# HGRN and mLSTM step on one core: weight splits and feature products moved from GpSimd to VectorE, small copies to ScalarE, and v's gate weights placed behind evictions

## The chip, the cores and the metric

The kernel runs on one core of a Trainium2 chip. The metric is the time of one execution on the device in microseconds (us). Before the change the median of three runs is 1189.55 us (1186.49 to 1191.88). Five engines work beside each other, each on its own queue: TensorE (PE: matmuls and transposes; its weight loads are shown as PEld), VectorE (DVE), ScalarE (ACT), GpSimd (POOL) and SyncE (SP, which here issues the DMAs).

## The reference

One layer of a hybrid decoder, for a prompt of 1024 tokens and 8 samples of 8 tokens (1088 token columns in all), model width 1024. After an RMSNorm one input projection of width 7168 gives the inputs of two mixers; both are causal recurrences over the tokens.

```python
proj = rmsnorm(x, g_norm) @ w_in
xm, zm, om, fh, qh, ih, zh = split(proj)             # 7 parts of 1024
# mLSTM, 4 heads, dk 128, dv 256
xc = silu(causal_conv(xm)); q = xc @ w_q; k = xc @ w_k; v = xm @ w_v      # per head
gates = concat(q, k, v) @ w_gate + b_gate            # input gate and forget gate of each head
hm = mlstm_scan(q, k, v, gates)                      # matrix memory C, normaliser n, stabiliser m
hm = (layernorm(hm) * sigmoid(om) + m_skip * xc) * silu(zm)
# HGRN2, 8 heads, dk = dv = 128
f = lb + (1 - lb) * sigmoid(fh); k = (1 - lb) * sigmoid(-fh); q = silu(qh)
oh = hgrn2_scan(q, k, ih, log f)                     # S_t = diag(f_t) S_(t-1) + k_t i_t ; o_t = S_t^T q_t
oh = rmsnorm(oh) * silu(zh)
y = rmsnorm(x + concat(hm, oh) @ w_out, g_final)
```

The new states of both mixers are outputs as well.

## The kernel before

A product of float32 accuracy is made of three matmuls: each operand is split into `hi`, a copy in a rounded 32-bit format, and `lo = raw - hi`. Lines 94, 95 and 96 are the three matmuls hi x hi, lo x hi, hi x lo of a projection, for tiles of 384, 384 and 320 token columns into the PSUM tile `mm`. The weights of the input projection come in 56 blocks of 128 columns. For each block one DMA on SP's queue brings `wraw` (three buffers), ScalarE casts `whi`, GpSimd subtracts `wlo`, both at L147 in `w_split`.

In time the program has these stages: the norm and split of x (to some 38 us); the front, which projects the mLSTM inputs, runs the conv (`front_conv`, sums `Y`), and makes v, q and k with the gate weights folded into the weights (`qkv_prep`, `front_v`, `front_qk`; to some 208 us); then a row of jobs H0 M0 H1 M1 H2 M2 H3 M3 H4 H5 H6 H7, where H is the scan of one HGRN head (`hgrn_main`) and M that of one mLSTM head (`mlstm_main`); and the output projection (from some 1020 us).

In `qkv_prep` v's gate weights take three steps on TensorE: four transposes of w_v (L395, evicted as `wT`), two matmuls with w_gate (L399, evicted as `gv`), two small transposes (L404), whose result VectorE splits into `wqh` and `wql`, columns of the weights of v (L406, L407). Between them only the dependences and the scheduler's costs set the place.

In the jobs TensorE's order is fixed by the code. `weave` runs a job as a generator whose `yield`s give the time of the other engines' work in us; between two yields it puts that much of the next job's input projection (the side blocks, "fillers" here), scaled by the projection's time over `HEAD[kind] + extra`. Each job takes exactly 48 pieces of the side work. VectorE, ScalarE, GpSimd and SP follow the scheduler's order, one in-order queue each.

An H job works in levels n = 1, 2, 4, 8, 16, 32, 64. For each level VectorE builds the factors `QK` from queries, keys and running products of f (`products`, L1016, L950; `Sf` L1019 and `f` L1021 carry the running products; level 1 uses `Q` L983, `K` L947, L998 to L1000). A burst of small matmuls of 32x32 blocks (L101) then gives the scores, and they are copied into the score matrix `A`, through the small tile `A32` for n up to 16. There are three bursts: level 1 and 2; `lower` (2, 4 and 8); `upper` (16, 32 and 64). After `upper` a predicated copy on VectorE fills `A32`, six copies (L1058 and L1060) bring A32 to A, and six copies on ScalarE (L1066) bring the rest from PSUM. TensorE's transposes L1123 follow; the second group of them takes the PSUM buffer that those copies read.

`mixed` finishes the mLSTM features of the job before: a DMA brings `xcr`, VectorE makes a fused product (L846), GpSimd multiplies by `zm` (L848), and a DMA stores it to `mixd`. It runs within the next H job, behind the products of the levels, as `late` work.

Of the kernel before, what the change touches and what calls it, by code (L numbers as in the profile page):

```python
# [13 lines left out]
ALU = mybir.AluOpType  # L14
# [16 lines left out]
def hybrid_step(  # L31
# [46 lines left out]
    def f32(ap):  # L78
        return ap.bitcast(F32)
# [61 lines left out]

    def w_split(key):
        raw = wq[key]
        hi = wp.tile([P, 1024], F32R, tag="whi", name=nm("whi"))
        lo = wp.tile([P, 1024], F32R, tag="wlo", name=nm("wlo"))
        wq[key] = (hi.rearrange("p (k c) -> p k c", c=P), lo.rearrange("p (k c) -> p k c", c=P))
        return S.copy(hi, raw), G.tensor_tensor(lo, raw, f32(hi), op=ALU.subtract)  # L147

# [11 lines left out]
    bidx = {b: i for i, b in enumerate(blocks)}  # L160

    def blk_load(i):
        if i < len(blocks):
            kind, j = blocks[i]
            o = boff[kind] + j * P
            return w_load(("w", i), w_in[0, :, o:o + P].rearrange("(k p) c -> p k c", p=P))

    def blk_split(i):
        if i < len(blocks):
            return w_split(("w", i))  # L170

# [201 lines left out]
    def vcols(w):  # L373

        return w[:, 512:1040].rearrange("p (a c) -> p a c", c=264)

    def qkv_prep(h):

# [13 lines left out]
        for b in range(2):  # L392
            for a in range(2):
                o, i = 512 + a * 256 + b * P, b * 2 + a
                PE.transpose(pt[:, i * P:(i + 1) * P], wr[:, o:o + P], ident)  # L395
        V.tensor_copy(wT[:, :512], pt)
        pg = ps_o()
        for b in range(2):
            PE.matmul(pg[:8, :256], lhsT=wgr[:, 8 + 2 * h + b, :], rhs=wT[:, b * 256:(b + 1) * 256],  # L399
                      start=b == 0, stop=b == 1)  # L400
        gv = sp.tile([P, 256], F32, tag="hn", name=nm("gv"), bufs=3)
        V.tensor_copy(gv[:8, :], pg[:8, :256])
        for a in range(2):
            PE.transpose(pg[:, 256 + a * 8:264 + a * 8], gv[:8, a * P:(a + 1) * P], ident[:8, :8])  # L404
        pgv = pg[:, 256:272].rearrange("p (a c) -> p a c", c=8)
# [35 lines left out]

    fr = {}

    def front_conv(h, fts):

        cw, cb = par("conv_w"), par("conv_b")
        items, st = [], []
        for ft in fts:
            XB = unit("XB")
# [6 lines left out]
            def evac(c, t0, n, ps, XB=XB, sv=sv, mh=mh, ml=ml):  # L456
                m = min(n, TP - t0)
                S.copy(mh[:, t0:t0 + m], ps[:, :m])
                S.copy(XB[:, 3 + t0:3 + t0 + m], ps[:, :m])  # L459
                V.tensor_tensor(ml[:, t0:t0 + m], ps[:, :m], f32(mh[:, t0:t0 + m]), op=ALU.subtract)  # L460
                if m < n:
                    S.copy(sv[:, :, 3:11], ps[:, m:n].rearrange("p (b c) -> p b c", c=8))
                    S.copy(twice(mh[:, TP:U]), once(ps[:, m:n]))
                    V.tensor_tensor(twice(ml[:, TP:U]), once(ps[:, m:n]), twice(f32(mh[:, TP:U])), op=ALU.subtract)
# [79 lines left out]
    def gate_scan():  # L544
# [20 lines left out]
        V.tensor_tensor_scan(m, t1, y, initial=0.0, op0=ALU.add, op1=ALU.max)  # L565
        yield 5.5
        G.memset(t1, 1.0)
# [12 lines left out]
        nc.sync.dma_start(out=o_sm[0].rearrange("b h -> h b"), in_=msl[0:4, :])  # L580
        yield 5.5
        ps = ps_o()
# [82 lines left out]
    def mlstm_main(h):  # L665
# [176 lines left out]
        def mixed(a):  # L842
# [4 lines left out]
                                   op0=ALU.mult, op1=ALU.add)  # L847
            G.tensor_tensor(xc[:, :T], xc[:, :T], d["zm"][a][:, :T], op=ALU.mult)  # L848
            nc.sync.dma_start(out=mixd[ft], in_=xc[:, :T])
# [77 lines left out]
    def hgrn_main(h):  # L927
# [11 lines left out]
        def fold(Kn, n, second, ns):  # L939

            Knv = Kn[:, :512].rearrange("p (r c) -> p r c", c=P)
            for odd in range(2):
# [3 lines left out]
                if n == 1:  # L946
                    i = (G if second else V).tensor_copy(dst, ksrc)  # L947
                else:
# [32 lines left out]
        Q1 = unit("Q1")  # L981
        G.tensor_copy(hv(Q1, T, 1)[:, :, 0, :], hv(q, T, 1)[:, :, 0, :])
        q1 = V.tensor_tensor(hv(Q1, T, 1)[:, :, 1, :], hv(q, T, 1)[:, :, 1, :], hv(f, T, 1)[:, :, 1, :], op=ALU.mult)  # L983
# [41 lines left out]
        def level_run(group):  # L1025
# [24 lines left out]
            for n, o in outs:  # L1050
                if n <= 16:
                    small_out(ps, o, LEVELS.index(n) + 1, n)
                    if n == 16:

                        for j in range(4):
                            a = A[32 * j:32 * j + 32, 32 * j:32 * j + 1]
                            dst = bass.AP(a.tensor, a.offset, [a.ap[0], [256, 4], [224 - 64 * j, 2], [1, 32]])
                            G.tensor_copy(dst, A32[32 * j:32 * j + 32, 0:256].rearrange("p (r e c) -> p r e c", e=2, c=32))  # L1058
                        for g in range(2):
                            G.tensor_copy(A[64 * g:64 * g + 32, TP + 32 * g:TP + 32 * g + 32],  # L1060
                                          A32[64 * g:64 * g + 32, 256:288])
                else:
# [7 lines left out]
        for n in (2, 4, 8):  # L1070
            lower.append(products(n))
            if late:
                with tc.issue_after(getattr(lower[-1][3], "ins", lower[-1][3])):
                    late.pop(0)()
                yield 1.8
            yield 3.3
# [38 lines left out]
        level_run(upper)  # L1115
        yield 2.0
        KDt = unit("KDt")
# [415 lines left out]
```

## Time and profile before

| | |
|---|---|
| median of 3 runs | 1189.55 us (1186.49 to 1191.88) |
| profiled execution | 1189.85 us, span 1188.1 us, mean granted clock 0.985 |
| TensorE | busy 1130.5 us (95%), 9251 matmuls |
| VectorE | 782.3 us (66%), 1447 instructions |
| ScalarE | 441.1 us (37%), 973 |
| GpSimd | 381.9 us (32%), 504 |
| GpSimd's splits L147 | 56 of 2495 ns, 139.7 us |
| GpSimd's multiply L848 | 8 of 2727 ns, 21.8 us |

How it is read: in the waits, "PE lv L101 <- DVE QK L950" means that TensorE's instruction of line 101, which writes tile `lv`, waited for VectorE's of line 950, which writes `QK`. In a timeline a row gives the start, the duration, engine, line, operation, tiles and shapes, how many such instructions follow each other, and in brackets the idle time ahead of them and what ended it. "PEclk" is the share of the full clock that TensorE was granted in a window. H0 runs from about 208 to 298 us, H1's part up to its transposes from 363 to 412, H2's from 494 to 543, H3's from 626 to 675, H4's from 757 to 811.

### The profile page before, as it was taken

To read this page: it belongs to the slowest core of one execution; us is meant where nothing else is said; L and a number is where in the kernel's file an instruction comes from. 1 tells how busy PE (TensorE), PEld (TensorE's weight loads), DVE (VectorE), ACT (ScalarE), POOL (GpSimd) and SP (SyncE) were. 2 spreads that over 40 slices of the span, in tenths; PEclk is the share of its full clock that TensorE was granted. 3 is DMA by queue.
4 is the path that set the end of the run, shared out by engine and by line. 5 is a ranking of instruction groups with operands and counts; after the bars stand their busy time and mean duration, and the time that the engine had idled before them with its cause. 6 is when DMAs were issued, how large, how long until landed. Compare 5 with 4: busy or idle time off the path is not lost.

```text
span 1188.1 us, 22927 instructions
## 1 busy us (share of the span) xinstructions
PE 1130.5 (95%) x9251; PEld 1062.1 (89%) x9251; DVE 782.3 (66%) x1447; ACT 441.1 (37%) x973; POOL 381.9 (32%) x504
## 2 busy tenths in 40 slices
PE   5889999979999999999999999989999999999997
PEld 5789999979999899998999899979999997877886
DVE  4665454395778767794678667795959587643543
ACT  5455454325431343225331453232232344343322
POOL 4352434132534344343534343443333211100000
PEclk9989999989999999999999999998999999999999
DMA  8134243222323242323224232321221155476652
GB/s 264 42 127 147 101 160 102 73 55 90 100 80 115 71 165 75 116 80 118 80 76 144 77 131 76 118 84 58 59 59 51 59 175 152 144 232 166 210 178 100
DMA packets 154061, 133.88 MB, mean 113 GB/s; under 512 B 11440, under 2 KB 130156, under 8 KB 153955
## 3 DMA queue, kind: packets, MB, share of 16 engines
q1 hardware_dynamic: 153954, 132.41, 35.8%
q8 instruction: 73, 1.20, 0.4%
q14 instruction: 34, 0.27, 0.1%
HBM read 93.96 MB, written 38.43 MB: 111 GB/s over the span
## 4 chain that ended last, share of the span: by engine, by line
PE 54%; DVE 13%; DMA 5%; ACT 2%; issue 2%; POOL 0%; SPq 0%; POOLq 0%; DVEq 0%; ACTq 0%
PE mm L94 14%; PE mm L96 14%; PE mm L95 14%; DVE QK L950 3%; DVE Sf L1019 2%; DVE f L1021 2%; DMA xcr<-xcd 2%; DMA woraw<-in_w_out 2%; PE o L1169 1%; DMA mraw<-mixd 1%; DVE QK L1016 1%; PE o L1188 1%; PE o L95 1%; PE o L94 1%; PE o L96 1%
## 5 line engine op out<-in xcount | busy, mean ns | idle before, releaser
L94 PE MATMUL mm<-XH,whi 128*128 128x384 f32 (+1 forms) x1344 | 454.0, 338 | 6.5 <-DVE z L890 6.2
L95 PE MATMUL mm<-XL,whi 128*128 128x384 f32 (+1 forms) x1344 | 442.1, 329 | 0.0
L96 PE MATMUL mm<-XH,wlo 128*128 128x384 f32 (+1 forms) x1344 | 441.7, 329 | 0.0
L94 PEld LDWEIGHTS mm<-XH,whi 128*128 128x128 f32 x1344 | 255.6, 190 | 10.3 <-DVE z L890 6.3
L95 PEld LDWEIGHTS mm<-XL,whi 128*128 128x128 f32 x1344 | 255.7, 190 | 1.7 <-issue 1.3
L96 PEld LDWEIGHTS mm<-XH,wlo 128*128 128x128 f32 x1344 | 255.0, 190 | 0.0
L147 POOL TENSOR_TENSOR wlo<-wraw,whi 128x1024 fp32r<-128x1024 f32 x56 | 139.7, 2495 | 184.9 <-ACT whi L147 184.4
L147 ACT CAST whi<-wraw 128x1024 fp32r<-128x1024 f32 x56 | 58.8, 1051 | 146.7 <-PE mm L95 126.5
L96 PE MATMUL mm<-XH,mlo 128*128 128x512 f32 x144 | 56.4, 392 | 2.0 <-DVE mlo L1282 2.0
L94 PE MATMUL mm<-XH,mhi 128*128 128x512 f32 x144 | 57.2, 397 | 0.5 <-ACT mhi L1281 0.5
L950 DVE TENSOR_TENSOR QK<-hk,Sf 128x256 f32<-128x256 f32 x96 | 56.2, 625 | 0.0
L95 PE MATMUL mm<-XL,mhi 128*128 128x512 f32 x144 | 56.1, 390 | 0.0
L1281 ACT CAST mhi<-mraw 128x1024 fp32r<-128x1024 f32 (+1 forms) x32 | 31.8, 996 | 61.6 <-PE mm L95 42.0
L1350 POOL TENSOR_TENSOR rs<-rs,mhalf 128x1 f32<-128x1 f32 (+1 forms) x9 | 4.9, 543 | 149.5 <-DVE rs L1349 149.5
L1282 DVE TENSOR_TENSOR mlo<-mraw,mhi 128x1024 fp32r<-128x1024 f32 (+1 forms) x32 | 36.9, 1154 | 23.8 <-ACT mhi L1281 23.8
L460 DVE TENSOR_TENSOR xml<-mm,xmh 128x384 fp32r<-128x384 f32 (+1 forms) x24 | 12.1, 508 | 57.8 <-ACT XB L459 48.8
L1019 DVE TENSOR_TENSOR Sf<-Sf,f 128x512 f32<-128x512 f32 (+1 forms) x48 | 46.5, 969 | 0.1
L882 DVE TENSOR_SCALAR f<-f,OML,LB 128x384 f32<-128x384 f32 (+1 forms) x24 | 32.1, 1338 | 19.5 <-ACT f L880 19.3
L1021 DVE TENSOR_TENSOR f<-f 128x512 f32<-128x512 f32 (+1 forms) x48 | 42.2, 879 | 0.8
L1060 POOL COPY A<-A 32x32 f32<-32x32 f32 x16 | 14.3, 891 | 85.2 <-DVE A L977 84.8
L96 PE MATMUL mm<-woh,mlo 128*128 128x512 f32 x96 | 37.5, 391 | 0.5 <-DVE mlo L1282 0.5
L94 PE MATMUL mm<-woh,mhi 128*128 128x512 f32 x96 | 37.4, 389 | 0.0
(350 smaller groups left out, 2221.7 us busy)
## 6 DMA issues: line engine op xcount, KB each, us to landing
wraw<-in_w_in SPq DMA_DIRECT2D x56, 512.0 KB, 4.2
woraw<-in_w_out SPq DMA_DIRECT2D x16, 512.0 KB, 5.3
mraw<-mixd SPq DMA_DIRECT2D x16, 512.0 KB, 5.4
mraw<-mixd SPq DMA_DIRECT2D x16, 448.0 KB, 3.8
xcd<-XB SPq DMA_DIRECT2D x8, 544.0 KB
qkd<-qk SPq DMA_DIRECT2D x16, 272.0 KB, 4.4
xcr<-xcd SPq DMA_DIRECT2D x8, 544.0 KB
mixd<-xcr SPq DMA_DIRECT2D x8, 544.0 KB, 2.7
```

The costliest lines, as they stand in the source:

```text
L94: PE.matmul(out, lhsT=lh, rhs=rh, start=first, stop=False)
L95: PE.matmul(out, lhsT=lh, rhs=rl, start=False, stop=False)
L96: PE.matmul(out, lhsT=ll, rhs=rh, start=False, stop=last)
L147: return S.copy(hi, raw), G.tensor_tensor(lo, raw, f32(hi), op=ALU.subtract)
L460: V.tensor_tensor(ml[:, t0:t0 + m], ps[:, :m], f32(mh[:, t0:t0 + m]), op=ALU.subtract)
L882: V.tensor_scalar(f[:, s], f[:, s], scalar1=OML[:, h:h + 1], scalar2=LB[:, h:h + 1], op0=ALU.mult, op1=ALU.add)
L950: i = V.tensor_tensor(dst, ksrc, ssrc, op=ALU.mult)
L1019: V.tensor_tensor(hv(Sf, W, n)[:, :, 0, :], hv(Sf, W, n)[:, :, 0, :], hv(f, W, n)[:, :, 1, n - 1:n].to_broadcast([P, ng, n]), op=ALU.mult)
L1021: V.tensor_tensor(hv(f, W, n)[:, :, 1, :], hv(f, W, n)[:, :, 1, :], hv(f, W, n)[:, :, 0, n - 1:n].to_broadcast([P, ng, n]), op=ALU.mult)
L1060: G.tensor_copy(A[64 * g:64 * g + 32, TP + 32 * g:TP + 32 * g + 32], A32[64 * g:64 * g + 32, 256:288])
L1281: S.copy(hi[:, :w * n], raw[:, :w * n])
L1282: V.tensor_tensor(lo[:, :w * n], raw[:, :w * n], f32(hi[:, :w * n]), op=ALU.subtract)
```

## The change

The subtraction of 22 of the 56 weight splits moves from GpSimd to VectorE: those issued within H jobs (the job's own z block and the first two blocks of the next job). So does the multiply by `zm` in `mixed`. ScalarE takes from GpSimd the even half of `Q`, the second key copies of level 1, and the copies A32 to A. The yields of the gate scan, of the late work and behind the upper burst grow, and HEAD and `extra` with them. `behind` ties each of the three TensorE steps of v's gate weights, by a dependence without a semaphore, to an eviction `xml` of the projection that runs beside them: the first, the one at a third, the one ahead of two thirds.

```diff
-    def w_split(key):
+    def w_split(key, eng=G):
...
-        return S.copy(hi, raw), G.tensor_tensor(lo, raw, f32(hi), op=ALU.subtract)
+        return S.copy(hi, raw), eng.tensor_tensor(lo, raw, f32(hi), op=ALU.subtract)
...
+    v_splits = {8 + 4 * j + n for j, (kind, _) in enumerate(jobs) if kind == "H" for n in (3, 4, 5)}
...
-            return w_split(("w", i))
+            return w_split(("w", i), V if i in v_splits else G)
...
+    def behind(i, r):
+        tc.add_manual_dep(getattr(i, "ins", i), getattr(r, "ins", r).name, mybir.DependencyInfo(
+            mybir.DependencyClass.NoSync, mybir.DependencyReason.DATA), reason="behind")
...
-                PE.transpose(pt[:, i * P:(i + 1) * P], wr[:, o:o + P], ident)
+                behind(PE.transpose(pt[:, i * P:(i + 1) * P], wr[:, o:o + P], ident), evs[0])
...
-            PE.matmul(pg[:8, :256], lhsT=wgr[:, 8 + 2 * h + b, :], rhs=wT[:, b * 256:(b + 1) * 256],
-                      start=b == 0, stop=b == 1)
+            behind(PE.matmul(pg[:8, :256], lhsT=wgr[:, 8 + 2 * h + b, :], rhs=wT[:, b * 256:(b + 1) * 256],
+                             start=b == 0, stop=b == 1), evs[len(evs) // 3])
...
-            PE.transpose(pg[:, 256 + a * 8:264 + a * 8], gv[:8, a * P:(a + 1) * P], ident[:8, :8])
+            behind(PE.transpose(pg[:, 256 + a * 8:264 + a * 8], gv[:8, a * P:(a + 1) * P], ident[:8, :8]),
+                   evs[2 * len(evs) // 3 - 1])
...
-                V.tensor_tensor(ml[:, t0:t0 + m], ps[:, :m], f32(mh[:, t0:t0 + m]), op=ALU.subtract)
+                evs.append(V.tensor_tensor(ml[:, t0:t0 + m], ps[:, :m], f32(mh[:, t0:t0 + m]), op=ALU.subtract))
...
-        yield 5.5
+        yield 6.5
...
-        yield 5.5
+        yield 6.5
...
-            G.tensor_tensor(xc[:, :T], xc[:, :T], d["zm"][a][:, :T], op=ALU.mult)
+            V.tensor_tensor(xc[:, :T], xc[:, :T], d["zm"][a][:, :T], op=ALU.mult)
...
-                    i = (G if second else V).tensor_copy(dst, ksrc)
+                    i = S.copy(dst, ksrc) if second else V.tensor_copy(dst, ksrc)
...
-        G.tensor_copy(hv(Q1, T, 1)[:, :, 0, :], hv(q, T, 1)[:, :, 0, :])
+        S.copy(hv(Q1, T, 1)[:, :, 0, :], hv(q, T, 1)[:, :, 0, :])
...
-                            G.tensor_copy(dst, A32[32 * j:32 * j + 32, 0:256].rearrange("p (r e c) -> p r e c", e=2, c=32))
+                            S.copy(dst, A32[32 * j:32 * j + 32, 0:256].rearrange("p (r e c) -> p r e c", e=2, c=32))
...
-                            G.tensor_copy(A[64 * g:64 * g + 32, TP + 32 * g:TP + 32 * g + 32],
-                                          A32[64 * g:64 * g + 32, 256:288])
+                            S.copy(A[64 * g:64 * g + 32, TP + 32 * g:TP + 32 * g + 32], A32[64 * g:64 * g + 32, 256:288])
...
-                yield 1.8
+                yield 2.6
...
         level_run(upper)
-        yield 2.0
+        yield 3.4
...
-    HEAD = {"H": 47.2, "M": 48.2}
+    HEAD = {"H": 48.6, "M": 48.2}
...
-                extra = 3.6
+                extra = 5.2
             if i == 0:
-                main, extra = with_gates(main, gates), 12.0
+                main, extra = with_gates(main, gates), 14.0
```

Line numbers of the changed kernel are larger: by 2 at L239 to L351, 7 or 8 from L395 to L407, 10 from L460 to L1060, and 9 behind that.

**VectorE in H1, from the scores of level 1 to the products of level 8.** `xcr` is `mixed`'s tile (two of them, 4046 and 4092), `QK_4085` level 4, `QK_4139` level 8. Before:

```order
L1019 TENSOR_TENSOR Sf_3937<-Sf_3937,f_3550 128x272x2
L977 COPY_PREDICATED A_539_3935<-mk_366,lv_3990 128x144
L1021 TENSOR_TENSOR f_3550<-f_3550 128x272x2
L950 TENSOR_TENSOR QK_4085<-hk_3551,Sf_3937 128x64x4
L950 TENSOR_TENSOR QK_4085<-hk_3551,Sf_3937 128x4x16x4
L952 TENSOR_TENSOR QK_4085<-hk_3551,Sf_3937 128x64
L1016 TENSOR_TENSOR QK_4085<-hq_3552,f_3550 128x544
L1019 TENSOR_TENSOR Sf_3937<-Sf_3937,f_3550 128x136x4
L1021 TENSOR_TENSOR f_3550<-f_3550 128x136x4
L846 SCALAR_TENSOR_TENSOR xcr_4092<-xcr_4092,PAR,om_2929 128x1088
L1016 TENSOR_TENSOR QK_4139<-hq_3552,f_3550 128x512
L950 TENSOR_TENSOR QK_4139<-hk_3551,Sf_3937 128x32x8
```

After (L856 is L846, L858 is L848, L960 is L950, L1026 is L1016, L1029 is L1019, L1031 is L1021):

```order
L987 COPY_PREDICATED A_539_3935<-mk_366,lv_3990 128x144
L856 SCALAR_TENSOR_TENSOR xcr_4046<-xcr_4046,PAR,om_2683 128x1088
L1026 TENSOR_TENSOR QK_4085<-hq_3552,f_3550 128x544
L1029 TENSOR_TENSOR Sf_3937<-Sf_3937,f_3550 128x136x4
L858 TENSOR_TENSOR xcr_4046<-xcr_4046,zm_3152 128x1088
L856 SCALAR_TENSOR_TENSOR xcr_4092<-xcr_4092,PAR,om_2902 128x1088
L1031 TENSOR_TENSOR f_3550<-f_3550 128x136x4
L147 TENSOR_TENSOR wlo_4109<-wraw_3949,whi_4108 128x1024
L858 TENSOR_TENSOR xcr_4092<-xcr_4092,zm_3353 128x1088
L1026 TENSOR_TENSOR QK_4139<-hq_3552,f_3550 128x512
L960 TENSOR_TENSOR QK_4139<-hk_3551,Sf_3937 128x32x8
L960 TENSOR_TENSOR QK_4139<-hk_3551,Sf_3937 128x4x8x8
```

Two multiplies (L858) and a split (L147) now stand ahead of the products of level 8; another split stands ahead of the last piece of `hq`, in front of all the levels, and a third ahead of the job's end.

**ScalarE in H1, from the scan's values to the copies that TensorE's transposes wait for.** `A_539` with `A_3933` are A and A32, `lv_4367` the PSUM tile of the upper burst. Before:

```order
L1102 CAST Vs_4330<-V_4311 128x128
L1106 ACTIVATE VH_4331<-Vs_4330,CF 128x128 x4
L1107 ACTIVATE VL_4332<-Vs_4330,CF 128x128 x4
L1066 COPY A_3933<-lv_4367 32x4x32 x4
L1066 COPY A_3933<-lv_4367 64x4x64 x2
L634 ACTIVATE om_4271<-mm_4348 128x384
```

After (L1075 is L1066):

```order
L1111 CAST Vs_4330<-V_4311 128x128
L1115 ACTIVATE VH_4331<-Vs_4330,CF 128x128 x4
L1116 ACTIVATE VL_4332<-Vs_4330,CF 128x128 x4
L1068 COPY A_3933<-A_539_3935 32x4x2x32 x3
L1068 COPY A_3933<-A_539_3935 32x4x64
L1075 COPY A_3933<-lv_4367 32x4x32 x4
L1075 COPY A_3933<-lv_4367 64x4x64 x2
L644 ACTIVATE om_4271<-mm_4348 128x384
```

The four copies A32 to A (L1068) stand ahead of the six copies out of PSUM. The two small ones (L1070) stand earlier, behind the evictions of z.

**TensorE in H1, between the upper burst and the transposes** (L1123, now L1132; `mm_4436` is a side block's tile of 320 columns):

```order
 L95 MATMUL mm_4436<-XL,whi_4108 128x320
 L96 MATMUL mm_4436<-XH,wlo_4109 128x320
-L1123 MATMUL lv_4447<-CF,iT_3553 128x128 x4
-L1123 MATMUL lv_4453<-CF,iT_3553 128x128 x4
-L1123 MATMUL o_4459<-CF,iT_3553 128x128
+L94 MATMUL mm_4436<-XH,whi_4108 128x320
+L95 MATMUL mm_4436<-XL,whi_4108 128x320
+L96 MATMUL mm_4436<-XH,wlo_4109 128x320
+L94 MATMUL mm_4436<-XH,whi_4108 128x320
+L95 MATMUL mm_4436<-XL,whi_4108 128x320
+L96 MATMUL mm_4436<-XH,wlo_4109 128x320
+L1132 MATMUL lv_4453<-CF,iT_3553 128x128 x4
```

Six more fillers stand ahead of the transposes. In the same way six fillers of the next tile now stand ahead of the lower burst.

**TensorE in the front, head 0, at the end of its second block's projection** (`mm_539`) and the start of v (`mm_618`):

```order
 L95 MATMUL mm_539<-XL,whi_167 128x320
 L96 MATMUL mm_539<-XH,wlo_168 128x320
-L404 MATMUL o_609<-CF,gv_612 128x8 x2
-L395 MATMUL o_848<-CF,wqkv_719 128x128 x4
+L406 MATMUL o_609<-wT_602,front_341 8x256 x2
+L411 MATMUL o_609<-CF,gv_612 128x8 x2
 L94 MATMUL mm_618<-wqh_376,xmh_385 128x264
 L94 MATMUL mm_630<-wqh_376,xmh_385 128x264
-L399 MATMUL o_854<-wT_847,front_341 8x256 x2
 L95 MATMUL mm_618<-wql_377,xmh_385 128x264
```

L399 (now L406), which stood at the start of the projection, now stands right ahead of L404 (now L411) and of v's first matmuls. Head 1's transposes and L399 (o_848, o_854) leave this place for the projection that follows.

More of the change, by code (lines that the diff above doesn't have):

```diff
@@ L442, in hybrid_step @@
     fr = {}
+    evs = []
     def front_conv(h, fts):
@@ L447, in front_conv @@
         items, st = [], []
+        evs.clear()
         for ft in fts:
```

## The prediction

> **What bounds the kernel now.** I read the page first, then the waits of TensorE, then the timeline of TensorE, VectorE, GpSimd and ScalarE inside one HGRN job, and last the table by windows of the clock. The page says who sets the time:
>
> ```profile
> PE 1130.5 (95%) x9251; PEld 1062.1 (89%) x9251; DVE 782.3 (66%) x1447; ACT 441.1 (37%) x973; POOL 381.9 (32%) x504
> ```
>
> TensorE is busy for 95% of the span, and the change takes no matmul away. What it can win is TensorE's waiting, and time in which TensorE runs at half clock. The waits of TensorE (us in total, times, longest):
>
> ```profile
> PE lv L1123 <- ACT A L1066: 10.5, 5, 3.2
> PE lv L101 <- DVE QK L950: 7.9, 4, 2.2
> PE mm L94 <- DVE z L890: 6.2, 1, 6.2
> ```
>
> The first two are the ends of the two halves of an HGRN job: the burst of small products (L101) that waits for the factors QK of level 8, and the transposes (L1123) that wait until ScalarE has copied the upper burst out of its PSUM tile. They fall in heads 0 to 4; H5 to H7 show none. One job, head 1, on TensorE:
>
> ```profile
> 387.80 0.48 PE L101 MATMUL lv<-QK 128*32 128x32 f32 x32 [1.97 <-DVE QK L950]
> ...
> 401.68 1.22 PE L101 MATMUL lv<-QK 128*32 128x32 f32 x96
> ...
> 403.98 0.31 PE L94 MATMUL mm<-XH,whi 128*128 128x320 f32 x1
> ...
> 404.86 0.60 PE L1123 MATMUL lv<-CF,iT 128*128 128x128 f32 x4
> 406.63 0.66 PE L1123 MATMUL lv<-CF,iT 128*128 128x128 f32 x4 [1.18 <-ACT A L1066]
> ```
>
> In head 0 the transposes wait less, so that 10.5 - 0.75 = 9.75 us of that row belong to H1 to H4:
>
> ```profile
> 274.69 0.66 PE L1123 MATMUL lv<-CF,iT 128*128 128x128 f32 x4 [0.75 <-ACT A L1066]
> ```
>
> The waits also cost clock. In the windows below the columns are length, busy us of PE, PEld, DVE, ACT, POOL, then PEclk. They are cut where the granted clock changes:
>
> ```profile
> 384.69:388.10 3.41, 1.44 (x114) 1.09 (x113) 3.41 (x3) 0.49 (x1) 2.77 (x2) 1.00 0.44 168
> 388.10:391.51 3.41, 3.41 (x32) 3.35 (x19) 3.38 (x8) 0.00 (x0) 0.00 (x0) 0.50 0.56 154
> 538.29:541.70 3.41, 3.41 (x15) 3.41 (x15) 0.58 (x2) 1.05 (x4) 0.00 (x0) 0.50 0.02 5
> 801.11:804.52 3.41, 2.56 (x11) 2.56 (x12) 1.09 (x3) 3.01 (x9) 0.25 (x1) 0.50 0.00 1
> 804.52:807.94 3.42, 3.42 (x16) 3.42 (x15) 0.30 (x1) 0.00 (x0) 0.00 (x0) 0.50 0.00 0
> 667.99:671.40 3.41, 1.59 (x12) 1.59 (x13) 0.00 (x0) 3.31 (x11) 1.11 (x3) 1.00 0.08 19
> 671.40:674.80 3.40, 3.40 (x29) 3.40 (x28) 1.92 (x6) 0.26 (x1) 0.00 (x0) 1.00 0.02 5
> ```
>
> After a window with 1.44 us of busy TensorE the next runs at 0.50; after one with 1.59 it does not. So a wait of 1.97 us already costs half of the next 3.41 us, 1.7 us. Such losses in H1 to H4: 1.7 (H1, 388.10), 1.7 (H2, 538.29), and in H4 half of 2.56 and of 3.42, 3.0; together 6.4 us.
>
> [...]
>
> **Why VectorE is late.** VectorE's timeline in H1, from the queries to the products of the next levels:
>
> ```profile
> 365.31 2.17 DVE L983 TENSOR_TENSOR Q<-hq,f 128x544 f32<-128x544 f32 x1
> ...
> 374.01 2.92 DVE L1019 TENSOR_TENSOR Sf<-Sf,f 128x544 f32<-128x544 f32 x1
> ...
> 379.24 0.71 DVE L1019 TENSOR_TENSOR Sf<-Sf,f 128x544 f32<-128x544 f32 x1
> ...
> 382.50 5.24 DVE L950 TENSOR_TENSOR QK<-hk,Sf 128x256 f32<-128x256 f32 x2
> ...
> 389.45 0.75 DVE L950 TENSOR_TENSOR QK<-hk,Sf 128x256 f32<-128x256 f32 x2
> ...
> 397.86 2.77 DVE L1021 TENSOR_TENSOR f<-f 128x512 f32<-128x512 f32 x1
> 400.66 1.29 DVE L1086 TENSOR_TENSOR hq<-hq,f 128x1088 f32<-128x1088 f32 x1
> ```
>
> The same operation on the same shape takes 2.92 and 0.71, 5.24 and 0.75. The long ones end 0.3 to 0.6 us behind the end of a GpSimd instruction:
>
> ```profile
> 364.50 2.39 POOL L147 TENSOR_TENSOR wlo<-wraw,whi 128x1024 fp32r<-128x1024 f32 x1 [0.96 <-ACT whi L147]
> ...
> 373.80 2.55 POOL L848 TENSOR_TENSOR xcr<-xcr,zm 128x1088 f32<-128x1088 f32 x1 [4.38 <-DVE xcr L846]
> 382.05 2.92 POOL L848 TENSOR_TENSOR xcr<-xcr,zm 128x1088 f32<-128x1088 f32 x1 [5.70 <-DVE xcr L846]
> 384.93 2.53 POOL L147 TENSOR_TENSOR wlo<-wraw,whi 128x1024 fp32r<-128x1024 f32 x1
> ...
> 397.69 2.39 POOL L147 TENSOR_TENSOR wlo<-wraw,whi 128x1024 fp32r<-128x1024 f32 x1
> ```
>
> These are the three splits and the two multiplies that the change takes from GpSimd. Held time up to the burst of level 8, with 0.71 as the free time of either 544-wide product: (2.17 - 0.71) + (2.92 - 0.71) + (5.24 - 0.75) = 8.16 us; behind it 2.77 - 0.7 = 2.1.
>
> **The change part by part, H1 to H4.** VectorE gets two splits and two multiplies ahead of level 8. A split's price is that of the same form in the tail, the multiply's that of L1086 above, 1.29:
>
> ```profile
> L1282 DVE TENSOR_TENSOR mlo<-mraw,mhi 128x1024 fp32r<-128x1024 f32 x16 | 19.6, 1224 | 22.4 <-ACT mhi L1281 22.4
> ```
>
> The first split can't start before GpSimd's did (364.50), ends at 365.72, and the query product behind it starts there, not at 364.79: 0.93. The second costs 1.22, the multiplies 2.58; together 4.73. So level 8 ends 8.16 - 4.73 = 3.4 us earlier, at 387.74 - 3.4 = 384.3. TensorE came to the burst at 387.80 - 1.97 = 385.83, and now comes six filler matmuls later (the larger HEAD and yields put them ahead of it). Six fillers took 404.86 - 403.98 = 0.88, so 386.7. The wait is gone, with 2.4 us to spare: 7.9 us won in the four heads. Ends: 0 if the held time went on, 7.9 if it goes; I take 7.9, since the long rows stand beside GpSimd's and the short ones don't.
>
> At the transposes, the chain is: end of the upper burst, one predicated copy on VectorE, then on ScalarE four copies A32 to A that came from GpSimd, now ahead of the six copies that TensorE waits for:
>
> ```profile
> 404.78 1.80 ACT L1066 COPY A<-lv 32x128 f32<-32x128 f32 x6
> ...
> L1066 ACT COPY A<-lv 64x256 f32<-64x256 f32 x16 | 5.9, 368 | 0.2
> ```
>
> The four of 32x256 have no row on ScalarE. Nearest is the 64x256 copy with the same 256 elements a row, 0.37; four make 1.5 (between 0, if they hide in a gap, and four of GpSimd's longest such copies, 4). After the burst (ends 402.90): some 0.5 for the predicated copy, 1.5, 1.80, sum 3.8. TensorE reaches the second group of transposes 406.63 - 1.18 - 402.90 = 2.55 after the burst now, plus 0.88 by the six new fillers, 3.4. A wait of 0.4 a head stays, 1.6 in all. So 9.75 - 1.6 = 8.1 is won here. VectorE itself is in time: the third split (1.22) takes the place of the held 2.1. On SP's queue the stores of mixd wait for the multiplies, and the next weight loads stand behind them:
>
> ```profile
> 376.38 8.93 SPq L849 DMA_DIRECT2D mixd<-xcr  x2
> 387.48 13.01 SPq L140 DMA_DIRECT2D wraw<-in_w_in  x2
> ```
>
> The first load starts at 387.48, right behind the split of 384.93, whose raw buffer it takes. With the split ended at 381.7 and the second multiply at 383.0 it starts about 4 us earlier: nothing lost, and nothing won, since no row of TensorE waits for a weight load there.
>
> With both waits small, no window falls under 1.59 us and the clock stays: 6.4. Sum H1 to H4: 7.9 + 8.1 + 6.4 = 22.4 us.
>
> **H0.** VectorE also runs the gate scan here and is itself the bound; TensorE stands 6.2 us at L94 for it.
>
> ```profile
> 242.82 2.36 DVE L571 TENSOR_TENSOR glf<-glf,gm 4x7 f32<-4x7 f32 x1
> ...
> 254.34 2.87 DVE L950 TENSOR_TENSOR QK<-hk,Sf 128x256 f32<-128x256 f32 x2
> ```
>
> Seven elements a row in 2.36 us is again waiting; without it some 0.2. With 2.87 - 0.75 = 2.1 that frees 4.3 us; two splits there cost 2.4. VectorE ends 1.9 earlier and TensorE with it. I take 2 (0 to 4). The wait at L94 itself shrinks by more, but TensorE then waits at the bursts.
>
> **Front.** The gate weights of v are put behind evictions. For head 0 the two matmuls L399 no longer come early (they wait 2.1 us there now, but the next matmul waits for an eviction ending as late, so I win nothing). Now the chain L399, copy gv, transposes L404, wqh, wql starts at the end of the projection, on VectorE between the conv's sums Y:
>
> ```profile
> 58.55 2.77 DVE L476 SCALAR_TENSOR_TENSOR Y<-XB,PAR,Y 128x1112 f32<-128x1112 f32 x1
> ...
> 61.88 0.56 PE L95 MATMUL mm<-wql,xmh 128*128 128x264 f32 x1 [2.18 <-DVE wql L407]
> 61.99 1.36 DVE L476 SCALAR_TENSOR_TENSOR Y<-XB,PAR,Y 128x1112 f32<-128x1112 f32 x1
> ```
>
> wql now stands behind one more Y (1.36) and wqh, so TensorE's 61.88 becomes about 63.4: a loss of 1.5 (ends: loss of 4 if another half-clock window is added, gain of 2 if the early wait goes). Heads 1 to 3 have other matmuls between the three steps and show no such wait: 0.
>
> **The rest.** H5 to H7: their transposes had no wait; ScalarE's chain ahead of them grows by 1.5 and the fillers ahead of them by 0.9 to 1.4: a loss of 0.1 to 0.6 each where nothing was to spare; I take 0.1 each, 0.3. The Q and K copies on ScalarE run beside VectorE's half of the same work, and replace GpSimd copies that held it: 0, kept out of the sum. The two copies of 32x32 wait at the head of ScalarE's queue for VectorE's last lower-level copy, with a cast and z's activation behind them; VectorE is earlier, so 0; without that lead, up to 1 us a head.
>
> Sum: 22.4 + 2 - 1.5 - 0.3 = 22.6. The profiled execution took 1189.85 us, which is 0.3 above the median, 1189.55; 1189.85 - 22.6 = 1167.
>
> **The rivals.** A measurement of this kernel can tell about 0.5%, 6 us, from no change: 1183.6 and 1195.5 are the bounds.
>
> *ScalarE's chain takes the place.* If the four copies cost GpSimd-like times, or ScalarE is late at them, the transposes wait as before: 8.1 is not won, nor the clock in H2 and H4 (1.7 + 3.0). 1167 + 12.8 = 1180. For it: they stand ahead of the copies that TensorE waits for. Against: rows of 0.25 to 0.37 us. Chance 0.2.
>
> *The clock does not follow.* Half-clock windows would stay, as if their cause weren't these waits: 22.6 - 6.4 = 16.2, 1173.6. [...] Against it stand the seven windows. Chance 0.1.
>
> *A wait for the cast.* The splits now block VectorE's queue until ScalarE's cast has run, and that waits for TensorE to free the buffer:
>
> ```profile
> 376.60 1.05 ACT L147 CAST whi<-wraw 128x1024 fp32r<-128x1024 f32 x1 [2.81 <-POOL xcr L848]
> ```
>
> The second split now stands four operations behind the start of the row 379.24 (that product 0.7, a multiply 1.3, the product of xcr as long, L1021 0.7: 4.0). That row starts at 379.24 - 3.7 + 0.9 = 376.5, so VectorE comes to the split at 380.5; the cast ends at 377.65. It must be 2.9 us later to hold VectorE at all, and 2.9 + 2.4 = 5.3 to reach TensorE; at 9 us the four heads lose 3.7 each and two half clocks stay, near 1185: no change that can be told. Chance 0.08.
>
> *Slower: VectorE becomes the bound.* If the long operations are long for another reason than GpSimd, nothing is freed and level 8 ends 4.73 - 0.88 = 3.85 us later against TensorE in each of H1 to H4: 15.4, plus 2.4 in H0, 1.5 in front and 1.7 for H3's new half clock: 21, 1211. It decides where less than 3.85 of the 8.16 is freed. Against: four long rows, each with GpSimd's end just ahead of its own. Chance 0.07.
>
> **How the numbers follow.** The forecast, 1167, has 0.55. Best ends together (no wait left at the transposes 1.6, H0 2 more, front 3.5 more) give 1160; ScalarE's rival with front's bad end gives 1183. The range 1159 to 1184 leaves out the last two rivals and a little beyond each end. Faster: 0.55 + 0.1 + most of 0.2, 0.83. Same: 0.1. Slower: 0.07.
>
> **What would show it.** Right: VectorE's L1019 and L950 of H1 at 0.7 throughout, the L101 wait for QK gone in H1 to H4, the wait of the transposes at 0 to 0.6 a head, no 0.50 window in H1 to H4, TensorE's wait for wql in front near 3.5. Wrong: long VectorE rows with GpSimd idle, a wait of TensorE for z or QK above 2 us in H1 to H4, or VectorE idle for whi.

## Result and the profile after

The changed kernel takes 1169.32 us in the median of four runs (1167.87 to 1171.67), against 1189.16 for the kernel before: a ratio of 0.9835, 95% interval 0.9806 to 0.9864. That is 19.8 us less; 1167 was forecast. The profiled executions were 1167.87 us (span 1166.1) and 1189.85 us (span 1188.1), 22 us apart. The page after, first part:

```profile
PE 1124.4 (96%) x9251; PEld 1057.3 (91%) x9251; DVE 748.0 (64%) x1477; ACT 469.6 (40%) x1045; POOL 260.5 (22%) x402
```

VectorE took over 22 splits of 1.22 us and 8 products of 1.29, 37 us of work, and is busy for 34 us less than before (782.3). Its other rows fell by some 71 us. Its timeline in H1 after, for the lines that stood there before:

```profile
370.19 0.72 DVE L1029 TENSOR_TENSOR Sf<-Sf,f 128x544 f32<-128x544 f32 x1
...
378.51 1.23 DVE L147 TENSOR_TENSOR wlo<-wraw,whi 128x1024 fp32r<-128x1024 f32 x1
379.65 1.29 DVE L858 TENSOR_TENSOR xcr<-xcr,zm 128x1088 f32<-128x1088 f32 x1
...
381.45 0.76 DVE L960 TENSOR_TENSOR QK<-hk,Sf 128x256 f32<-128x256 f32 x2
...
396.96 0.28 DVE L1112 TENSOR_TENSOR Vs<-V,Vs 128x128 fp32r<-128x128 f32 x1
...
399.68 0.30 DVE L987 COPY_PREDICATED A<-mk,lv 128x128 f32<-128x128 uint8 x1 [2.33 <-PE lv L101]
```

The product of 2.92 us is 0.72, the pair of 5.24 is 0.76. The last row is the one to remember: at the end of the job VectorE now stands idle for 2.33 us and waits for TensorE's upper burst. Before, the same copy stood in line behind VectorE's other work, with no idle time ahead of it:

```profile
403.58 0.29 DVE L977 COPY_PREDICATED A<-mk,lv 128x128 f32<-128x128 uint8 x1
```

The idle time is called slack below: by about so much VectorE could be later without holding up TensorE. TensorE's waits after:

```profile
PE lv L1132 <- ACT A L1075: 5.9, 8, 2.2
PE mm L94 <- DVE wqh L414: 3.3, 1, 3.3
PE lv L101 <- DVE QK L1026: 2.3, 1, 2.3
```

The wait for QK of level 8 is gone in H1 to H4; the 2.3 left is H0's upper burst. In H1 VectorE ends level 8 at 382.21, and TensorE comes to the lower burst at 386.19, 4.0 us later:

```profile
386.19 1.16 PE L101 MATMUL lv<-QK 128*32 128x32 f32 x112
```

The wait for z in H0 fell from 6.2 to 1.0. At the transposes 0.48 a head stays in H1 to H4, and H5 to H7 now have 0.5 to 0.7. In H1:

```profile
400.01 1.65 ACT L1068 COPY A<-A 32x256 f32<-32x256 f32 x4 [1.09 <-DVE A L987]
401.68 1.82 ACT L1075 COPY A<-lv 32x128 f32<-32x128 f32 x6
403.53 0.50 ACT L644 ACTIVATE om<-mm 128x384 f32<-128x384 f32 x1
```

```profile
403.56 0.66 PE L1132 MATMUL lv<-CF,iT 128*128 128x128 f32 x4 [0.48 <-ACT A L1075]
```

In the windows (length, busy us of PE, PEld, DVE, ACT, POOL, PEclk) H1 to H4 have no half clock any more (the second row is H2's stretch). H0 has one such window with 3.27 us busy; before it had two, from 254.98 to 261.81, the first with 0.07 us busy and the second with 3.41:

```profile
266.41:269.82 3.41, 3.27 (x40) 3.10 (x41) 3.41 (x7) 1.28 (x4) 0.00 (x0) 0.50 0.00 0
```

```profile
480.00:530.00 50.00, 49.52 (x580) 48.19 (x573) 39.21 (x80) 16.96 (x47) 2.91 (x9) 1.00 0.36 118
```

Where the time came from, by the trace, between the same counts of the projection's matmuls (L94 to L96) in both kernels: from the first to the 1152nd (the front and some 20 us of H0) 211.0 us before and 212.3 after; to the 1440th (the rest of H0) 74.3 and 73.1; to the 2160th (M0, H1) 144.5 and 139.9; to the 2736th (M1, H2) 120.7 and 114.4; to the 3312th (M2, H3) 115.6 and 111.3; from there to the 5472nd (H4 to the output) 494.5 and 487.2. H1 and what follows gives 22.6, H0 1.2; the front costs 1.3, and TensorE started 0.5 later.

### The profile page after: what moved, and what is told of

It is laid out like the page before. It is cut to its first block, busy times and chain, and to the rows that moved or that the text cites. A ratio compares the mean times of both kernels' runs of the same rounds, so it can differ in the third digit from the quotient of the medians.

```text
span 1166.1 us, 22935 instructions
## 1 busy us (share of the span) xinstructions
PE 1124.4 (96%) x9251; PEld 1057.3 (91%) x9251; DVE 748.0 (64%) x1477; ACT 469.6 (40%) x1045; POOL 260.5 (22%) x402
## 4 chain that ended last, share of the span: by engine, by line
PE 67%; ACT 4%; DMA 2%; DVE 2%; issue 1%; POOLq 0%; SPq 0%; DVEq 0%; ACTq 0%
PE mm L94 18%; PE mm L96 18%; PE mm L95 18%; PE lv L101 2%; ACT A L1075 1%; PE o L1178 1%; ACT A L1068 1%; PE o L1197 1%; DMA woraw<-in_w_out 1%; PE o L94 1%; PE o L95 1%; PE o L96 1%; PE o L1200 1%; DMA mraw<-mixd 1%; PE lv L712 1%
## 5 line engine op out<-in xcount | busy, mean ns | idle before, releaser
L94 PE MATMUL mm<-XH,whi 128*128 128x384 f32 (+1 forms) x1344 | 452.2, 337 | 3.2 <-DVE xml L470 2.0
L96 PE MATMUL mm<-XH,wlo 128*128 128x384 f32 (+1 forms) x1344 | 440.1, 328 | 0.0
L94 PEld LDWEIGHTS mm<-XH,whi 128*128 128x128 f32 x1344 | 254.2, 189 | 6.9 <-DVE xml L470 2.2
L96 PEld LDWEIGHTS mm<-XH,wlo 128*128 128x128 f32 x1344 | 253.7, 189 | 0.0
L147 POOL TENSOR_TENSOR wlo<-wraw,whi 128x1024 fp32r<-128x1024 f32 x34 | 83.1, 2446 | 108.3 <-ACT whi L147 108.2
L147 ACT CAST whi<-wraw 128x1024 fp32r<-128x1024 f32 x56 | 58.8, 1051 | 104.8 <-PE mm L95 85.3
L944 POOL MEMSET A<- 128x288 f32 x8 | 2.7, 343 | 248.2 <-ACT A L1068 248.2
L94 PE MATMUL mm<-XH,mhi 128*128 128x512 f32 x144 | 57.2, 397 | 0.5 <-ACT mhi L1290 0.5
L96 PE MATMUL mm<-XH,mlo 128*128 128x512 f32 x144 | 56.3, 391 | 0.7 <-DVE mlo L1291 0.7
L96 PE MATMUL mm<-woh,mlo 128*128 128x512 f32 x96 | 37.5, 390 | 0.4 <-DVE mlo L1291 0.4
L94 PE MATMUL mm<-woh,mhi 128*128 128x512 f32 x96 | 37.4, 389 | 0.0
L95 PE MATMUL mm<-wol,mhi 128*128 128x512 f32 x96 | 37.4, 389 | 0.0
L486 DVE SCALAR_TENSOR_TENSOR Y<-XB,PAR,Y 128x1112 f32<-128x1112 f32 x24 | 36.8, 1533 | 0.3
L199 POOL TENSOR_SCALAR oss<-oss 128x4 f32<-128x4 f32 (+1 forms) x24 | 4.6, 194 | 143.6 <-DVE oss L1148 143.6
```

What stands on the lines that cost most here:

```text
L94: PE.matmul(out, lhsT=lh, rhs=rh, start=first, stop=False)
L95: PE.matmul(out, lhsT=lh, rhs=rl, start=False, stop=False)
L96: PE.matmul(out, lhsT=ll, rhs=rh, start=False, stop=last)
L147: return S.copy(hi, raw), eng.tensor_tensor(lo, raw, f32(hi), op=ALU.subtract)
L486: V.scalar_tensor_tensor(Y[:, :1112], XB[:, j:j + 1112], cw[:, 8 * j + ft:8 * j + ft + 1], Y[:, :1112], op0=ALU.mult, op1=ALU.add)
```

## Experiments

All ratios are to the kernel before, run on the same chip. Two theories stood against each other at first: VectorE was held up by GpSimd's instructions beside it (the prediction's), or the new yields, which put fillers ahead of TensorE's bursts, carry the gain.

**The yields, taken away and alone.**

```diff
-        yield 6.5              # twice, gate scan
+        yield 5.5
-                yield 2.6      # late
+                yield 1.8
-        yield 3.4              # behind level_run(upper)
+        yield 2.0
-    HEAD = {"H": 48.6, ...     # extra 5.2 and 14.0
+    HEAD = {"H": 47.2, ...     # extra 3.6 and 12.0
```

> The changed kernel with the yields, HEAD and extra of before, all else as changed. Theory (TensorE's waits ended because VectorE is no longer held by GpSimd; the yields only add 0.88 us of fillers ahead of each burst): VectorE ends level 8 at 382.2 and TensorE came to the lower burst at about 386 in head 1, a slack near 3.9 us, so 0.88 less of it leaves no wait for QK; at the transposes the wait of 0.48 a head becomes about 1.3 in seven heads, +6 us: 1175. No half-clock window in H1 to H4. Rival (the larger yields carry the gain): the waits for QK come back, about 1180 to 1185.

Measured: 1178.74 us, ratio 0.9912 (0.9893 to 0.9930). No wait for QK came back in H1 to H4. The wait at the transposes did:

```profile
PE lv L1132 <- ACT A L1075: 13.7, 8, 4.4
```

It is 1.36 a head in H1 to H4, 0.48 plus the 0.88 of six fillers, as expected, 1.2 to 1.5 in H5 to H7, and 4.4 in H0, which has three half-clock windows (270.69 to 280.93) where the changed kernel has one. The yields are worth 9.4 us, 4 more than expected; by the profiled executions, 11 us apart, H0 took 2.3 us longer, H1 to H3 4.8, H4 and what follows 5.6.

> The kernel before with only the new yields, HEAD and extra. Theory: VectorE stays held by GpSimd, so the waits for QK shrink only by the six fillers, from 1.97 to about 1.1 a head, and those at the transposes by 0.88 a head: 7 us less waiting, and one or two half-clock windows fewer (1.7 each): about 1180. VectorE's long rows (2.92, 5.24 us) stay. Rival (yields carry the gain): about 1170. Rival (moves carry it all): 1189.

Measured: 1186.38 us, ratio 0.9991 (0.9971 to 1.0010). Alone they bring nothing that can be told.

```profile
PE lv L1123 <- ACT A L1066: 11.5, 7, 2.7
PE lv L101 <- DVE QK L950: 6.1, 4, 2.4
```

6.1 and 11.5 us against 7.9 and 10.5 before: fillers ahead of a burst move TensorE's wait to the next place while VectorE is as late as ever. So the yields pay only once VectorE is early.

**The splits and products back on GpSimd, both.**

```diff
-            return w_split(("w", i), V if i in v_splits else G)
+            return w_split(("w", i))
-            V.tensor_tensor(xc[:, :T], xc[:, :T], d["zm"][a][:, :T], op=ALU.mult)
+            G.tensor_tensor(xc[:, :T], xc[:, :T], d["zm"][a][:, :T], op=ALU.mult)
```

> The changed kernel with the 22 splits and the 8 multiplies back on GpSimd; yields, ScalarE's copies and the place of v's gate weights as changed. Theory (VectorE held by GpSimd): the long rows of VectorE come back, level 8 ends about 3.4 us later in H1 to H4, which uses up the slack of 3.9 us, so the wait for QK is 0 to 1 us a head; H0, where VectorE is the bound, loses 1.9: 1171 to 1176. Rival (VectorE's 37 us of added work cost as much as the hold): 1169 or less.

Measured: 1190.40 us, ratio 1.0020 (1.0002 to 1.0037): the whole gain is gone. The expectation was far too low. Its part on the wait for QK held, there is none in H1 to H4, but it stopped at that burst:

```profile
PE lv L1132 <- ACT A L1075: 19.5, 8, 4.4
```

The transposes wait 3.5 us in each of H1 to H3 and 4.4 in H4. In H1, VectorE and then ScalarE:

```profile
402.79 0.29 DVE L1112 TENSOR_TENSOR Vs<-V,Vs 128x128 fp32r<-128x128 f32 x1
...
403.09 0.30 DVE L987 COPY_PREDICATED A<-mk,lv 128x128 f32<-128x128 uint8 x1
```

```profile
403.11 1.28 ACT L1116 ACTIVATE VL<-Vs,CF 128x128 fp32r<-128x128 f32 x4 [3.41 <-DVE Vs L1112]
404.30 1.62 ACT L1068 COPY A<-A 32x256 f32<-32x256 f32 x4
405.95 1.82 ACT L1075 COPY A<-lv 32x128 f32<-32x128 f32 x6
```

Vs starts at 402.79 and not at 396.96 (of the 5.8, some 1.2 is from earlier in the run). VectorE has no gap between level 8 and Vs, so its lateness runs on to ScalarE's queue: VL, four copies, six copies, transposes. I had taken the slack at the lower burst for the slack of the job. The slack is the 2.33 us of the row L987 above; here the same row, at 403.09, has no idle time ahead of it.

**Each alone.**

> The changed kernel with the 22 splits alone back on GpSimd. Theory (what counts is when VectorE ends the whole job, since ScalarE's copies and the transposes follow its last product): each of the three splits of a job holds VectorE for about 1.5 to 2.2 us in place of 1.22 of its own, 1.9 a job; H0 to H4 lose 1.9 each and a half-clock window or two: about 1179. Rival (a split on GpSimd costs no more than one on VectorE): 1169.

Measured: 1175.37 us, ratio 0.9883 (0.9851 to 0.9914), 6 us over the changed kernel; the two intervals just overlap. By the same counts of matmuls H0 takes 79.4 us in place of 73.1, H1 to H3 take 1.3 more, and what follows 0.7. So the expected 1.9 a head did not come: from H1 on little is lost, and H0 loses 6.3, with a wait of 3.8 at its transposes and three half-clock windows (277.53 to 287.77) where the changed kernel has one. That the splits cost H0 6.3 is not shown: with splits and products both back it took 74.8, with one such window.

> The changed kernel with the 8 feature products alone back on GpSimd. Theory: two of them hold VectorE for about 4.4 us a job in H1 to H4 in place of 2.6 of its own, so 1.8 later each, 7 in all and perhaps a half-clock window: about 1177. Together with the splits' part that makes most of the 21 us that both cost. Rival: 1169, the whole is in the splits, or in both together.

Measured: 1171.27 us, ratio 0.9861 (0.9829 to 0.9892), 2 us over the changed kernel, which the intervals do not tell from none. VectorE's last copy in H1, with the splits back and then with the products back:

```profile
406.40 0.30 DVE L987 COPY_PREDICATED A<-mk,lv 128x128 f32<-128x128 uint8 x1 [0.39 <-PE lv L101]
```

```profile
400.27 0.30 DVE L987 COPY_PREDICATED A<-mk,lv 128x128 f32<-128x128 uint8 x1 [0.28 <-PE lv L101]
```

6 and 2 do not add up to the 21 of both; from H1 on, by the counts of matmuls, it is 1.9 and 3.3 against 20.7. The slack explains that: of 2.33 us, 0.39 and 0.28 are left. Counted from the 1872nd matmul of L94 to L96, Vs comes 15.6 us later in the changed kernel, 17.5 with the splits back, 17.6 with the products back and 20.2 with both. Either delay, some 2 us, is inside the slack (waits of 0.8 to 1.0 at the transposes of H1 to H3, in place of 0.48); the 4.6 of both is not, and 3 of it reach TensorE in each head. With both back the waits at the transposes of H1 to H4 are 13.0 us longer, and four half-clock windows stand behind them, in H1, H3 and H4 (two), of up to 1.7 us each: together nearly the 20.7.

**What holds VectorE: products or time of GpSimd.** Both kernels put extra work on GpSimd behind each feature product, into a scratch tile `scr` of 128x544; nobody reads its result.

```diff
             V.tensor_tensor(xc[:, :T], xc[:, :T], d["zm"][a][:, :T], op=ALU.mult)
+            for _ in range(4):                                          # gps_reads
+                G.tensor_tensor(scr, xc[:, 0:544], xc[:, 544:T], op=ALU.mult)
```

```diff
+            G.tensor_copy(scr[:, 0:1], xc[:, 0:1])                      # gps_fills
+            for _ in range(8):
+                G.memset(scr, 0.0)
```

> The changed kernel, and behind each of the eight feature products on VectorE four products on GpSimd, 128x544, that read the feature tile in SBUF and write a scratch tile which nobody reads. Theory (a GpSimd product that reads SBUF holds VectorE's two-operand products): each four, some 5.2 us, keep VectorE from about that much work in H1 to H4, level 8 ends 7 to 9 us later against a slack of 3.9, so TensorE waits 3 to 5 us a head for QK and loses clock: about 1185 to 1195. Rival (GpSimd's work beside VectorE costs nothing): 1169.

Measured: 1203.71 us, ratio 1.0127 (1.0109 to 1.0145), 34 us over the changed kernel with not one instruction more on VectorE, whose 1477 instructions are busy for 779.5 us in place of 748.0. The loss is larger than expected, and in another place: TensorE waits 0.5 us a head at the upper burst and 4.5 at the transposes, the end of the job once more. GpSimd and VectorE in H1 (the first of the eight products is in the row from 377.40 on, but ended only at 384.05):

```profile
377.40 18.47 POOL L861 TENSOR_TENSOR scr<-xcr 128x544 f32<-128x544 f32 x8 [12.24 <-DVE xcr L859]
```

```profile
382.06 0.77 DVE L963 TENSOR_TENSOR QK<-hk,Sf 128x256 f32<-128x256 f32 x2
...
386.29 3.06 DVE L963 TENSOR_TENSOR QK<-hk,Sf 128x256 f32<-128x256 f32 x2
```

> As the kernel with added GpSimd products (1203.7 us), but behind each feature product GpSimd copies one column of the feature tile, so that it starts at the same place, and then fills the scratch tile eight times, 128x544, without reading SBUF; some 5.4 us of GpSimd time each, as long as the four products. Theory (it is GpSimd's reads of SBUF that hold VectorE's two-operand products): no hold, 1169 to 1171, VectorE's copies perhaps held. Rival (any GpSimd instruction holds VectorE, or the tile's longer life costs): 1195 to 1205.

Measured: 1172.34 us, ratio 0.9861 (0.9843 to 0.9880).

```profile
378.21 5.49 POOL L860 COPY scr<-xcr 128x1 f32<-128x1 f32 x1 [12.22 <-DVE xcr L859]
383.76 4.83 POOL L862 MEMSET scr<- 128x544 f32 x8
```

```profile
383.57 0.55 DVE L904 TENSOR_TENSOR z<-z,mm 128x384 f32<-128x384 f32 x1
...
385.37 0.76 DVE L964 TENSOR_TENSOR QK<-hk,Sf 128x256 f32<-128x256 f32 x2
```

Beside 4.83 us of fills the pair takes 0.76; beside products it takes 3.06. Over the whole run VectorE's 1477 instructions are busy for 747.4 us, against 748.0 in the changed kernel. So GpSimd's products hold VectorE's, and GpSimd's time as such does not: the prediction's central reason is shown. The fills differ from the products in two ways, they read nothing and compute little. The one-column copy reads, and computes nothing either; in H1 it took 5.49 us beside VectorE's products the first time and 0.29 the second, where eight fills took 4.83 together. That speaks for the reading, which is not tested apart. The kernel takes 3 us more than the changed one, but their intervals overlap, so that a small cost of the fills is neither shown nor excluded.

**v's gate weights.**

```diff
     def behind(i, r):
-        tc.add_manual_dep(...)
+        return
```

> The changed kernel without the three dependences of v's gate weights. Theory: the front loses 1.8 us by them (head 0's gate weights late), so 1167.5, with the waits for wT, wqh and wql of before (2.1, 1.4, 2.2). Rival (the dependences save something in heads 1 to 3): 1169 or more.

Measured: 1170.44 us, ratio 0.9845 (0.9829 to 0.9860): the same as the changed kernel within both intervals. The waits of before are back, as expected:

```profile
PE mm L95 <- DVE wql L414: 2.2, 1, 2.2
PE o L405 <- DVE wT L402: 2.1, 1, 2.1
PE mm L94 <- DVE wqh L413: 1.4, 1, 1.4
```

They replace 3.3 for wqh, 2.0 for an eviction, 1.4 for gv and 0.6 for wql. No difference between the two places can be told.

**ScalarE's copies.** First their order, then their engine.

```diff
                     if n == 16:
-                        ...                  # the copies A32 to A
...
+            if any(n == 16 for n, o in outs):    # behind the copies out of PSUM
+                ...
```

> The changed kernel, ScalarE's six copies out of the upper burst's PSUM tile written ahead of the four copies A32 to A. Theory: the first can start at the burst's end and take 1.82, so TensorE's waits at the transposes (2.19 in H0, 0.48 to 0.71 in H1 to H7, 5.9 in all) go: about 1164. Rival (the four copies only move ahead of the next eviction, and that one becomes late): 1169.

Measured: 1166.00 us, ratio 0.9809 (0.9788 to 0.9831): 3 us won of 5 expected. The waits at the transposes are gone but 0.55 in H0. What is late next, in TensorE's waits and on VectorE, in a profiled execution of 1171.04 us:

```profile
PE o L1227 <- DVE osq L1149: 5.3, 4, 2.0
```

```profile
416.10 2.19 DVE L687 SCALAR_TENSOR_TENSOR DT<-RB,COLS,CF 128x128 f32<-128x128 f32 x8 [2.32 <-DMA RB<-rd]
```

VectorE waits 2.3 us for a row that the next mLSTM job loads, and the norm of the H job stands behind it. That this took the missing 2 us is not shown: the profiled execution is the longest of five (the others took 1163.5 to 1166.6), and TensorE's wait for osq comes and goes among the kernels (0.8 us in all in the changed one's profile).

```diff
-                            S.copy(dst, A32[32 * j:...])            # and the two 32x32 copies
+                            G.tensor_copy(dst, A32[32 * j:...])
```

> The changed kernel with the copies A32 to A (six a job) back on GpSimd, the Q and K copies left on ScalarE. Theory (ScalarE's four copies, 1.65, stand ahead of the six that TensorE waits for): GpSimd makes them beside, the waits at the transposes go as with the six copies first (1166.0): 1165 to 1167. Rival (GpSimd's copies hold VectorE or come late, as before the change): 1172 or more.

Measured: 1160.22 us, ratio 0.9761 (0.9738 to 0.9784): 9 us faster than the changed kernel, 5 more than expected. GpSimd and ScalarE in H1:

```profile
396.49 1.70 POOL L1068 COPY A<-A 32x256 f32<-32x256 f32 x4 [8.40 <-DVE A L987]
```

```profile
396.46 1.82 ACT L1075 COPY A<-lv 32x128 f32<-32x128 f32 x6 [1.09 <-DVE A L987]
```

The two sets run side by side. VectorE has just ended its work of the job and runs nothing from 396.43 to 400.82, so GpSimd's copies hold nobody there. One wait at the transposes is left, 2.0 in H0, and no window between 65 and 1154 us is at half clock. By the counts of matmuls the spans, 8.2 us apart, differ so: H4 and what follows took 3.7 us less than in the changed kernel and H1 to H3 1.0 less, 4.7 together, of which the waits at the transposes there made 3.7; H0 took 1.6 less, the front 0.3, and TensorE started 1.6 earlier. For the last three no row shows the copies as the cause: in H0 the wait for QK is 2.34 us in both kernels, and only the half-clock window behind it is missing here (last section). So about half of the 9 us falls where the copies act, close to the 2 to 4 expected.

> The changed kernel with all copies back on GpSimd: A32 to A, and the Q and K copies of level 1; splits and feature products stay on VectorE. Theory (VectorE runs about 2.3 us ahead of TensorE at a job's end): the Q and K copies hold VectorE for some 1 to 1.5 us a job, inside that slack in H1 to H7; H0, where VectorE is the bound, loses 1: 1160 to 1162, so the whole move of copies to ScalarE was not needed. Rival (the Q and K copies on GpSimd cost as the splits did): 1165 or more.

Measured: 1161.62 us, ratio 0.9780 (0.9753 to 0.9807), not to be told from the last. So no gain from moving the Q and K copies is seen, and with the A copies on ScalarE, ahead of the six, the kernel takes 9 us more.

**Two together.** The six copies first, and head 0's gate weights without `behind`:

```diff
+    def late_gv(h):
+        return behind if h else (lambda i, r: None)
...                                  # late_gv(h) in place of behind at the three steps
```

> The changed kernel with the six copies first, and the dependences of v's gate weights left out in head 0 alone. Theory: both gains, 5.9 + 1.8: about 1162. Rival (one takes the other's place): 1164 to 1167.

Measured: 1163.39 us, ratio 0.9786 (0.9771 to 0.9800). The front takes as long as in the changed kernel (212.4 and 212.3 us by the counts above), so nothing came from head 0. What is left is the kernel with the six copies first, measured a second time: 5.9 us under the changed kernel, where the first measurement gave 3.3. Its interval overlaps with that of the A copies on GpSimd, which has the lowest median; so the order of ScalarE's copies may be worth as much as their engine.

## Why the prediction was right

*VectorE is held by GpSimd.* Right and shown: a pair of VectorE's products took 3.06 us beside added products and 0.76 beside fills, and 21 us were lost with splits and products back.

*The waits for QK, 7.9.* All four are gone, as worked out. The margin is 4.0 us in H1 and not 2.4: the sum of held time left out VectorE's own copies of level 1 (K 1.18 and Sf 1.22 us before, 0.49 and 0.44 after).

*The transposes, 9.75 to 1.6.* 1.9 is left. The chain came out in H1 as written: predicated copy, four copies of 1.65 (1.5 estimated), six of 1.82, and a wait of 0.48 (0.4).

*The clock, 6.4.* No window of H1 to H4 is at half clock; the four heads and what follows gave 22.6 where 22.1 was forecast with the clock counted, and 15.7 without. The size 6.4 holds for the profiled execution alone, since the same wait costs clock or not by where it falls (last section).

*H0, 2.* It gave 1.2. The 6.2 for z became 1.0, but 2.3 at the upper burst and 2.2 at the transposes came in its place, as said ahead in kind. The clock gave nothing here: one half-clock window with TensorE at work stands on either side (258.40 before, 266.41 after).

*Front, a loss of 1.5.* Between the kernels it is 1.3, but the step is not borne out: the same code of the front took 211.0 and 211.8 us in two kernels without the dependences and 213.3 in the third, and 209.5 to 213.5 with them. A term of 1.5 lies within that spread, and was mis-sized or nothing; which, stays open. The half-clock windows alone differ: the front has three before, four after, and two to four among the other kernels. So it is chance that this term came out so near. Its sign came in part: TensorE waits 3.3 us where near 3.5 was forecast, but for wqh, and only 0.6 for wql.

*H5 to H7, a loss of 0.3.* Their transposes wait 1.75 in all, 0.52 to 0.71 each: the upper end of the 0.1 to 0.6 that was written, where 0.1 was taken.

*What the sum did not see.* It took VectorE's slack from the first burst, and ScalarE's copies as given. The true margin was 2.33 us at the job's end, and the change with the A copies left on GpSimd gains 28 us and not 20.

## What to carry to other kernels

Where one engine's instructions are long at some places and short at others for the same shape, look at what runs beside them on the other engine before counting its load: work moved onto the busier engine can make it less busy (VectorE here 748.0 us in place of 782.3). Follow lateness to the end of the chain, not to the first wait: the slack is where the engine itself stands idle for the one that bounds the kernel. And test the parts of a change apart, since a harmful one can hide within a gain (the A copies on ScalarE, 9 us here). Parts that each cost next to nothing can cost much together, when each uses up the same slack (6 and 2 us here, and 21 together).

## What the runs showed of the hardware

*The hold works in both directions.* In each of H1 to H4 of the kernel with fills, GpSimd's first copy of one column was kept for 5.49 us (in H1 from 378.21 on), while seven instructions of VectorE with two SBUF operands followed each other without a gap; it ended right behind the start of L904 (383.57), an instruction with one operand in PSUM. The first of the added products waited in the same way, 6.65 us, and ended 1.3 us behind such an instruction's start (382.73). After that one GpSimd product and one or two VectorE instructions alternate, 1.41 to 1.70 us each on GpSimd. But the second copy of one column took 0.29 us (at 388.65), beside a pair of such products that runs from 388.47. So a dense stretch of VectorE can keep GpSimd out for long, and does not always; what decides is not shown.

*A fill is not free beside every instruction.* VectorE's copy Sf of level 1 takes 0.44 us in the changed kernel, with nothing on GpSimd. Where GpSimd copies K and then fills its part of Sf beside it, before the change and with all copies back, it takes 1.18 to 1.28 in 15 of 16 heads (0.65 in H3 before the change), and ends in those 15 some 0.30 us behind the end of the fill. So a fill seems to hold VectorE's copy, though not its products; no run tests it apart.

*Clock is lost behind windows that are only in part idle.* The half-clock stretches of each trace begin whole multiples of 3.41 us apart (between 200 and 1140 us at 254.98, 388.10, 538.29 and 801.11 before the change, at 266.41 after). In all fourteen traces, from 200 to 1140 us, 28 windows of this grid at full clock were followed by one at 0.50; they held 0 to 1.54 us of busy TensorE (0.54, 1.44, 0.78 and 0.94 before the change, 1.14 after). All others held 1.54 or more (at least 1.59 before the change, at least 2.08 after it). The nearest on either side are the window at 419.64 with the six copies first, which half clock followed, and that at 782.76 with the products back, which it did not:

```profile
419.64:423.05 3.41, 1.54 (x9) 1.02 (x8) 1.76 (x7) 3.38 (x5) 1.25 (x3) 1.00 0.04 15
782.76:786.17 3.41, 1.54 (x13) 1.30 (x12) 0.00 (x0) 3.27 (x11) 0.34 (x1) 1.00 0.01 2
```

So a wait of some 2 us costs up to 1.7 us more (half of 3.41) if it falls into one window, and in the case below nothing, where it was split over two: the wait of 2.34 us for QK in H0, in the changed kernel (ahead of the row 266.41) and, two rows, with the A copies on GpSimd.

```profile
262.98:266.40 3.42, 1.14 (x66) 0.69 (x64) 3.39 (x8) 2.81 (x9) 0.00 (x0) 1.00 0.52 148
```

```profile
259.83:263.24 3.41, 2.37 (x73) 1.90 (x71) 3.38 (x8) 1.98 (x7) 3.25 (x4) 1.00 0.82 236
263.24:266.65 3.41, 2.02 (x42) 1.93 (x43) 3.41 (x9) 1.37 (x5) 0.31 (x2) 1.00 0.02 4
```

In the front this limit does not hold: the changed kernel's window from 37.72 to 41.13 was busy for 2.62 us, and the next ran at 0.50.
